# Where a sum over three chunks stands among the products of the following chunk, in the dense stage of a decoder layer

## The chip, the cores and the metric

The kernel runs as one program on 1 core of a Trainium2 chip. The metric is the device time of one execution in microseconds (us), lower is better. The engines are named as the profile names them: PE is TensorE (PEld its weight load), DVE is VectorE, ACT is ScalarE, POOL is GpSimd and SP is SyncE, which issues most of the transfers. Each engine works through its own instructions in the order in which they stand there.

## The reference

A decoder layer over 1024 tokens of width 1024: two attention-like mixers, and then a product-key expert layer, which is the part that matters here. For each token 8 heads pick 16 of 16384 experts each; every expert is one row of a table `u` and one row of a table `v`.

```python
u_sel = jnp.take(u_tab, idx, axis=0)                # rows of the chosen experts
h = jnp.einsum('bthkd,btd->bthk', u_sel, xb)
a = (jax.nn.gelu(h.astype(jnp.float32)) * g).astype(xb.dtype)
return jnp.einsum('bthk,bthkd->btd', a, jnp.take(v_tab, idx, axis=0))
```

## The kernel before

The tokens are 8 blocks of 128. A first part (to about 1490 us) does the mixers and chooses the experts. The rest, to which the change belongs, does the expert layer in two ways side by side.

**Fetched blocks.** For 3 of the blocks (5, 6, 7) `fetch` gathers the rows of the chosen experts from the tables (an indirect DMA that POOL issues, L954), and DVE does one instruction of 128x1024 on each (L992 for `u`, L979 for `v`). These steps are dealt out along the dense work by `pace`.

**Dense blocks.** For the other 5 blocks (640 tokens) every expert is computed, and a gate, zero for the experts that were not chosen, multiplies the result. The 16384 experts are 128 chunks of 128. For chunk `c`:

- `split_u` and `split` bring in the chunk's rows of `u` and `v` (`raw`, 512 KB each, 3 buffers, issued by SP on L845), and write each as a rounded high part (`uh`, `vh`: ACT, L846) and a low part (`ul`, `vl`: POOL, L847; DVE for the first chunks). A `raw` buffer is free again when POOL has made the low part. There are 2 buffers for `u` and `CH + 1` = 4 for `v`.
- `products` multiplies `u` with the tokens (`dhT`, held in full) into two PSUM tiles `h` of 320 tokens each: the two halves. Each is 24 matmuls of 128x320 (8 pieces of the contraction, and three matmuls high-high, high-low, low-high for each, L138 to L140). There are 3 buffers for `h`.
- `gated` does gelu (ACT, L116), the multiplication with the gates (DVE, L897; the gates come in as `gg` and `gw`, issued by SP on L875 and L885), and the split into `ah` (ACT, L899) and `al` (DVE, L900). It is written one chunk later than the products that it reads.
- `outs` is the sum: for three chunks (`CH = 3`) at a time, `ah`, `al` of 5 token blocks times `vh`, `vl`, in 10 PSUM tiles `yo` of 128x512 with 3 buffers, 9 matmuls each (three for each chunk, the last chunk's three last), and DVE adds each tile to `y` (L911). The buffers of `v` of the three chunks are free when the last tile is done.

The order of the instructions on each engine is not the order of the text. A scheduler lays it out ahead of time from its own picture of when things are ready; the order of the text says only who goes first where several are ready. POOL alone keeps the order of the text (`manual_schedule`).

In what follows a *sum* is `outs` of one group of three chunks, and the *last chunk* of a group is the one whose products end last: chunks 2, 5, ..., 125.

Of the kernel before, what the change touches and what calls it, by code (L numbers as in the profile page):

```python
# [55 lines left out]
def layer(ctx: ExitStack, tc: tile.TileContext, a: dict, out: bass.AP):  # L56
# [79 lines left out]
    def mm3(o, l, r, start, stop):  # L136

        T.matmul(o, l[0], r[0], start=start, stop=False)  # L138
        T.matmul(o, l[0], r[1], start=False, stop=False)  # L139
        T.matmul(o, l[1], r[0], start=False, stop=stop)  # L140
# [22 lines left out]
    def main():  # L163
# [139 lines left out]
        def group(b0, b1):  # L303
# [322 lines left out]
            def build(b, jf, gg):  # L626
# [36 lines left out]
                for t1 in range(0, P, TB):  # L663
                    hot = hp.tile([P, 4, TB // 2, P, 2], BF16, name="hot", tag="zs", bufs=NZS)
                    io = iota.unsqueeze(1).to_broadcast([P, TB // 2, P, 2])
                    of = lambda k: part[:, k, t1:t1 + TB].rearrange("p (a i) -> p a i", i=2).unsqueeze(2) \
                        .to_broadcast([P, TB // 2, P, 2])
                    V.tensor_tensor(hot[:, 0], io, of(1), op=OP.is_equal)
                    V.tensor_tensor(hot[:, 3], io, of(0), op=OP.is_equal)
                    for u in range(3):  # L670
                        V.tensor_tensor(hot[:, 1 + u], hot[:, 3], of(2 + u), op=OP.mult)
                    made.append((t1, hot))
                    if len(made) == NZS:
                        products()
                    yield 1.0
                while made:
                    products()
                    yield 0.0
# [132 lines left out]
        with ExitStack() as g:  # L811
            nbd = len(DENSE)
            CH = 3
# [20 lines left out]
            def pace(cost):  # L834
                nonlocal due
                due += cost
                while due > 0:
                    due -= PACE
                    next(side, None)

            def split(pool, name, src, bufs, E=G):
                raw = wp.tile([P, D], F32, name="raw", bufs=3)
                hi = pool.tile([P, D], F32R, name=name + "h", bufs=bufs)
                lo = pool.tile([P, D], F32R, name=name + "l", bufs=bufs)
                DQ.dma_start(raw, src)  # L845
                step["split"] = A.copy(hi, raw).ins.name  # L846
                E.tensor_sub(lo, raw, hi)  # L847
                return hi, lo

            def split_u(c):  # L850
                hi, lo = split(wp, "u", a["peer_uT"][c].rearrange("p k e -> p (k e)"), 2, V if c < AHEAD else G)
                return [t.rearrange("p (k e) -> p k e", e=P) for t in (hi, lo)]

            def products(u):

                halves = []
                for t0 in range(0, ND, TH):
                    p = ps.tile([P, 512], F32, name="h", bufs=3)[:, 0:TH]
                    for k in range(KT):
                        mm3(p, (u[0][:, k], u[1][:, k]),  # L860
                            (hT[0][:, k, t0:t0 + TH], hT[1][:, k, t0:t0 + TH]), k == 0, k == KT - 1)
                    halves.append(p)
                return halves

            wide = {}

# [36 lines left out]
            def outs(parts):  # L903
                for b in range(nbd):
                    bs = slice(b * P, (b + 1) * P)
                    for f in range(2):
                        p = ps.tile([P, 512], F32, name="yo", bufs=3)
                        ds = slice(f * 512, f * 512 + 512)
                        for u, ((ah, al), (vh, vl)) in enumerate(parts):
                            mm3(p, (ah[:, bs], al[:, bs]), (vh[:, ds], vl[:, ds]), u == 0, u == len(parts) - 1)  # L910
                        V.tensor_tensor(y[:, b, ds], y[:, b, ds], p, op=OP.add)  # L911
                        pace(0.65 * len(parts))

            u = split_u(0)
            parts, last = [], None
            for c in range(NKEY + 1):
                if c < NKEY:
                    v = split(up, "v", a["peer_v"][c * P:(c + 1) * P], CH + 1, V if c < AHEAD else G)
                    un = split_u(c + 1) if c + 1 < NKEY else None
                    p = products(u)  # L920
                    u = un
                if c == 0:
                    for b in range(nbd):
                        DQ.dma_start(y[:, b], d_x1[DENSE[b]])
                if last is not None:
                    parts.append((gated(c - 1, last[0]), last[1]))
                if c < 2:
                    for _ in islice(first, None if c else H):
                        pass
                last = (p, v)  # L930
                pace(1.4 * nbd)
                if len(parts) == CH:
                    outs(parts)
                    parts = []
            if parts:
                outs(parts)
            for b in range(nbd):
# [6 lines left out]
    def fetch(blocks, decode, row, ahead, pool, bank):  # L944
# [20 lines left out]
        for b, table in work:  # L965
# [41 lines left out]
            had[b] = h  # L1007

    main()


# [56 lines left out]
```

## Time and profile before

| | us |
|---|---|
| median of 3 runs | 3417.93 (3412.2 to 3424.95) |
| the profiled execution, its own time | 3410.79 |
| its span, first to last instruction | 3409.0 |
| PE busy in the span | 3211.9 (94%) |
| DVE busy | 2665.7 (78%) |
| POOL busy | 2191.6 (64%) |
| ACT busy | 1296.9 (38%) |

Matmuls are pipelined: a record lasts longer than the distance to the start of the next one, so a busy PE is not PE at its peak, and the distance from start to start is what one matmul costs in a row of them. The granted clock (PEclk) is a share of the full 2.4 GHz. A wait is put down to the engine that released it last.

### The profile page before, as it was taken

The page shows a single profiled execution, that of the slowest core. Times are in us where ns is not written, and L with a number is a line of the kernel's source. Part 1 is how long each engine was busy: PE and PEld are TensorE (multiplying, and loading weights), DVE is VectorE, ACT ScalarE, POOL GpSimd, SP SyncE. Part 2 cuts the span into 40 slices and gives each one's busy share as a digit, 9 for nine tenths or more (in the row PEclk, how much of TensorE's full clock was granted, in tenths as well). Part 3 has the DMA queues.
Part 4 walks back from the last instruction along what each step waited for, and adds up shares of the span by engine and source line. Part 5 has one row for each costly group of instructions (what it writes and reads, how often), then busy time and mean ns, then how long its engine had stood idle before and what let it go on. Part 6 is the DMA issues. An engine that isn't in the chain of part 4 may idle for free.

```text
span 3409.0 us, 56377 instructions
## 1 busy us (share of the span) xinstructions
PE 3211.9 (94%) x20194; PEld 2936.4 (86%) x20194; DVE 2665.7 (78%) x6080; ACT 1296.9 (38%) x2440; POOL 2191.6 (64%) x1514
## 2 busy tenths in 40 slices
PE   7899999999889999978999999999999999999999
PEld 7799988999877899877888898888888888888887
DVE  5746996557997787899887878777787777778877
ACT  5565465554466755321222222222222222222221
POOL 3353177887888874015777767676767777777774
PEclk9999999999999999989999999999999999999999
DMA  7787555777645399667888889898889888888986
GB/s 218 214 243 254 168 135 124 152 169 171 129 77 119 68 182 183 169 244 261 319 297 303 302 310 323 300 330 296 320 304 328 316 307 317 315 311 321 327 303 240
DMA packets 625305, 832.81 MB, mean 244 GB/s; under 512 B 226176, under 2 KB 467456, under 8 KB 625024
## 3 DMA queue, kind: packets, MB, share of 16 engines
q1 hardware_dynamic: 459136, 426.29, 40.7%
q0 software_dynamic: 165888, 402.92, 36.7%
q8 instruction: 158, 2.59, 0.3%
q14 instruction: 123, 1.01, 0.1%
HBM read 757.03 MB, written 72.02 MB: 243 GB/s over the span
## 4 chain that ended last, share of the span: by engine, by line
PE 52%; DVE 17%; POOL 11%; DMA 7%; issue 7%; ACT 2%; another core or an unknown queue 0%; SPq 0%; POOLq 0%; DVEq 0%; ACTq 0%
POOL d_G L773 8%; PE yo L140 5%; PE yo L138 5%; PE h L140 5%; PE h L138 5%; PE yo L139 5%; PE h L139 5%; PE mm L138 5%; PE mm L139 5%; PE mm L140 4%; DVE row L992 4%; DVE g_p L979 3%; DMA raw<-in_peer_v 3%; POOL row L954 2%; DVE y L911 2%
## 5 line engine op out<-in xcount | busy, mean ns | idle before, releaser
L773 POOL DMA_INDIRECT d_G<-g_gate,g_idx x384 | 727.1, 1894 | 235.2 <-issue 114.2
L138 PE MATMUL h<-dhT,uh 128*128 128x320 f32 x2048 | 640.7, 313 | 26.3 <-ACT uh L846 15.4
L140 PE MATMUL h<-dhT,ul 128*128 128x320 f32 x2048 | 631.1, 312 | 15.2 <-POOL ul L847 9.3
L139 PE MATMUL h<-dhT,uh 128*128 128x320 f32 x2048 | 639.2, 312 | 0.0
L954 POOL DMA_INDIRECT row<-in_peer_u,g_idx x384 | 365.8, 953 | 422.0 <-ACT uh L846 190.6
L138 PE MATMUL yo<-vh,ah 128*128 128x512 f32 x1280 | 504.3, 399 | 61.7 <-ACT ah L899 42.9
L979 DVE SCALAR_TENSOR_TENSOR g_p<-row,g_h,g_p 128x1024 f32<-128x1024 f32 x384 | 492.7, 1283 | 48.3 <-DMA row<-in_peer_v,g_idx 41.3
L139 PE MATMUL yo<-vl,ah 128*128 128x512 f32 x1280 | 503.9, 396 | 1.6 <-POOL vl L847 1.6
L954 POOL DMA_INDIRECT row<-in_peer_v,g_idx x384 | 361.0, 940 | 218.1 <-DVE g_p L979 127.4
L992 DVE SCALAR_TENSOR_TENSOR row<-row,g_p 128x1024 f32<-128x1024 f32 x384 | 461.3, 1214 | 50.2 <-DMA row<-in_peer_u,g_idx 36.3
L140 PE MATMUL yo<-vh,al 128*128 128x512 f32 x1280 | 488.6, 394 | 0.0
L236 DVE TENSOR_TENSOR wl<-raw,wh 128x512 fp32r<-128x512 f32 x440 | 312.6, 713 | 192.9 <-ACT wh L235 179.8
L235 ACT CAST wh<-raw 128x512 fp32r<-128x512 f32 x528 | 326.1, 620 | 335.8 <-PE mm L140 101.4
L138 PEld LDWEIGHTS h<-dhT,uh 128*128 128x128 f32 x2048 | 391.5, 191 | 41.2 <-ACT uh L846 15.5
L140 PEld LDWEIGHTS h<-dhT,ul 128*128 128x128 f32 x2048 | 388.9, 191 | 24.4 <-POOL ul L847 11.0
L139 PEld LDWEIGHTS h<-dhT,uh 128*128 128x128 f32 x2048 | 391.2, 191 | 7.3
L911 DVE TENSOR_TENSOR y<-y,yo 128x512 f32<-128x512 f32 x430 | 287.7, 682 | 118.2 <-PE yo L140 72.9
L847 POOL TENSOR_TENSOR vl<-raw,vh 128x1024 fp32r<-128x1024 f32 x125 | 302.1, 2417 | 88.9 <-ACT vh L846 87.1
L138 PEld LDWEIGHTS yo<-vh,ah 128*128 128x128 f32 x1280 | 242.0, 190 | 119.5 <-ACT ah L899 48.3
L899 ACT CAST ah<-h 128x320 fp32r<-128x320 f32 x256 | 108.9, 426 | 529.4 <-DVE h L897 285.1
L847 POOL TENSOR_TENSOR ul<-raw,uh 128x1024 fp32r<-128x1024 f32 x125 | 301.3, 2411 | 7.4 <-ACT uh L846 7.4
L140 PEld LDWEIGHTS yo<-vh,al 128*128 128x128 f32 x1280 | 241.8, 190 | 49.1
(239 smaller groups left out, 7046.2 us busy)
## 6 DMA issues: line engine op xcount, KB each, us to landing
raw<-in_w_in SPq DMA_DIRECT2D x312, 256.0 KB
raw<-in_peer_uT SPq DMA_DIRECT2D x128, 512.0 KB
raw<-in_peer_v SPq DMA_DIRECT2D x128, 512.0 KB
d_G<-zero SPq DMA_DIRECT2D x24, 1024.0 KB
raw<-in_peer_w_q SPq DMA_DIRECT2D x96, 256.0 KB
d_B<-sl SPq DMA_DIRECT2D x32, 512.0 KB
gg<-d_G SPq DMA_DIRECT2D x128, 128.0 KB
gw<-d_B SPq DMA_DIRECT2D x32, 512.0 KB
```

What stands on the lines that cost most here:

```text
L138: T.matmul(o, l[0], r[0], start=start, stop=False)
L139: T.matmul(o, l[0], r[1], start=False, stop=False)
L140: T.matmul(o, l[1], r[0], start=False, stop=stop)
L235: A.copy(hi, raw)
L236: on["lo"][0](lo, raw, hi)
L773: d = G.indirect_dma_start(out=d_G[g], out_offset=bass.IndirectOffsetOnAxis(ap=to[:, s:s + 1], axis=0), in_=gg[:, s:s + 1], in_offset=None ...
L847: E.tensor_sub(lo, raw, hi)
L899: A.copy(ah[:, t], q)
L911: V.tensor_tensor(y[:, b, ds], y[:, b, ds], p, op=OP.add)
L954: d = G.indirect_dma_start(out=t, out_offset=None, in_=a["peer_v" if u else "peer_u"], in_offset=bass.IndirectOffsetOnAxis(ap=g_idx[b][:, ...
L979: V.scalar_tensor_tensor(acc, t, h[:, s:s + 1], acc, op0=OP.mult, op1=OP.add)
L992: V.scalar_tensor_tensor(t, t, 1.0, x, op0=OP.mult, op1=OP.mult, accum_out=h[:, s:s + 1])
```

## The change

`products` becomes a generator that gives out one half at a time. In the loop over the chunks the sum of a full group stood at the end of a pass, behind all of that chunk's products and the gating. It now stands in the next pass, between the first half of that chunk's products and the issue of that chunk's `v` and the next chunk's `u`; the second half follows them. Nothing is computed that was not computed before.

```diff
             def products(u):
-                halves = []
                 for t0 in range(0, ND, TH):
                     p = ps.tile([P, 512], F32, name="h", bufs=3)[:, 0:TH]
                     for k in range(KT):
                         mm3(p, (u[0][:, k], u[1][:, k]),
                             (hT[0][:, k, t0:t0 + TH], hT[1][:, k, t0:t0 + TH]), k == 0, k == KT - 1)
-                    halves.append(p)
-                return halves
+                    yield p
...
             for c in range(NKEY + 1):
                 if c < NKEY:
+                    half = products(u)
+                    p = [next(half)]
+                    if len(parts) == CH:
+                        outs(parts)
+                        parts = []
                     v = split(up, "v", a["peer_v"][c * P:(c + 1) * P], CH + 1, V if c < AHEAD else G)
                     un = split_u(c + 1) if c + 1 < NKEY else None
-                    p = products(u)
+                    p += list(half)
                     u = un
...
                 last = (p, v)
                 pace(1.4 * nbd)
-                if len(parts) == CH:
-                    outs(parts)
-                    parts = []
             if parts:
                 outs(parts)
```

What the scheduler makes of it is shown at three places. Lines of the changed kernel from L853 on are two lower (`gg` L873, `ah` L897).

The first is PE behind the products of chunk 80, the last chunk of its group (`h_29753` is its second half; `h_29813`, `h_29838` and, after, `h_29801`, `h_29838` are the halves of chunk 81; `ah_29868` belongs to chunk 80). Before:

```order
L140 MATMUL h_29753<-dhT0_18841,ul_29639 128x320
L138 MATMUL h_29813<-dhT0_18841,uh_29723 128x320 [waits DVE_49]
L139 MATMUL h_29813<-dhT1_18842,uh_29723 128x320
L140 MATMUL h_29813<-dhT0_18841,ul_29724 128x320 [waits Pool_49]
...
L138 MATMUL h_29838<-dhT0_18841,uh_29723 128x320 [waits DVE_49]
...
L140 MATMUL yo_29888<-vh_29632,al_29782 128x512
L138 MATMUL yo_29888<-vh_29717,ah_29868 128x512 [waits Activation_49]
```

After:

```order
L140 MATMUL h_29753<-dhT0_18841,ul_29664 128x320
L138 MATMUL h_29801<-dhT0_18841,uh_29748 128x320 [waits DVE_49,Activation_49]
L139 MATMUL h_29801<-dhT1_18842,uh_29748 128x320
L138 MATMUL yo_29913<-vh_29742,ah_29868 128x512 [waits Activation_49]
L139 MATMUL yo_29913<-vl_29743,ah_29868 128x512 [waits Pool_49]
...
L138 MATMUL h_29838<-dhT0_18841,uh_29748 128x320 [waits DVE_49]
L139 MATMUL h_29838<-dhT1_18842,uh_29748 128x320
L140 MATMUL yo_29913<-vh_29742,al_29869 128x512
...
L140 MATMUL h_29801<-dhT0_18841,ul_29749 128x320 [waits Pool_49]
```

The first matmul that needs `ah` of chunk 80 stood behind both halves of chunk 81; it now stands behind two matmuls of chunk 81.

The second is SP at the same place (`gg_30087` is the gates of chunk 81, the `raw` of `in_peer_v` next to it the `v` of chunk 81). Before:

```order
L845 DMA raw_29722<-in_peer_uT 128x1024 [waits DMAHW1_49,Pool_49]
L845 DMA raw_29801<-in_peer_v 128x1024 [waits DMAHW4_49,Pool_49]
L875 DMA gg_30087<-d_G0_131 128x256 [waits DMAHW3_49,DMAHW2_49,DVE_49]
L875 DMA gg_30087<-d_G1_132 128x128
L885 DMA gw_30482<-d_B_133 128x2x512 [waits DVE_49]
```

After:

```order
L845 DMA raw_29747<-in_peer_uT 128x1024 [waits DMAHW1_49,Pool_49]
L873 DMA gg_30087<-d_G0_131 128x256 [waits DMAHW3_49,DMAHW2_49,DVE_49]
L873 DMA gg_30087<-d_G1_132 128x128
L883 DMA gw_30482<-d_B_133 128x2x512 [waits DVE_49]
L845 DMA raw_29826<-in_peer_v 128x1024 [waits DMAHW4_49,Pool_49]
```

The load of `v` of chunk 81 moved behind three loads of gates that wait for DVE.

The third is ACT at chunk 104, also the last of its group (`vh` is that of chunk 105; `h_32890`, after `h_32878`, is the first half of chunk 104, `ah_33030` what becomes of it). Before:

```order
L846 CAST uh_32885<-raw_32884 128x1024 [waits DMAHW1_49,Pool_49]
L899 CAST ah_32943<-h_32830 128x320 [waits DVE_49,Activation_49]
L846 CAST vh_32964<-raw_32963 128x1024 [waits DMAHW3_49]
L116 ACTIVATE h_32890<-h_32890 128x320 [waits PE_49]
L899 CAST ah_33030<-h_32890 128x320 [waits DVE_49]
```

After:

```order
L897 CAST ah_32943<-h_32830 128x320 [waits DVE_49,Activation_49]
L846 CAST uh_32910<-raw_32909 128x1024 [waits DMAHW1_49,Pool_49]
L116 ACTIVATE h_32878<-h_32878 128x320 [waits PE_49]
L846 CAST vh_32989<-raw_32988 128x1024 [waits DMAHW5_49]
L897 CAST ah_33030<-h_32878 128x320 [waits DVE_49]
```

Gelu of chunk 104 moved ahead of the cast of `vh`, and the cast to `ah` still stands behind it.

## Rows read from the trace of the kernel before

**Rows 1.** The page: its first line.

```profile
span 3409.0 us, 56377 instructions
```

**Rows 2.** Windows: stretch, its us, busy us of each engine, PEclk, DMA share, GB/s.

```profile
1754.00:3409.00 1655.00, 1588.92 (x8738) 1433.85 (x8736) 1283.59 (x1935) 421.63 (x688) 1165.79 (x896) 0.99 0.86 309
```

**Rows 3.** Waits of PE, 1754 to 3409: us in total, times, longest.

```profile
PE yo L138 <- ACT ah L899: 37.2, 16, 5.9
```

**Rows 4.** Timeline of PE, chunk 98: start, us, line; in brackets idle before, releaser.

```profile
2949.66 0.39 PE L140 MATMUL yo<-vh,al 128*128 128x512 f32 x1
...
2963.12 0.31 PE L138 MATMUL h<-dhT,uh 128*128 128x320 f32 x1
2963.27 0.31 PE L139 MATMUL h<-dhT,uh 128*128 128x320 f32 x1
2966.65 0.96 PE L138 MATMUL yo<-vh,ah 128*128 128x512 f32 x3 [3.07 <-ACT ah L899]
```

**Rows 5.** Timeline of POOL, the same place.

```profile
2949.94 2.42 POOL L847 TENSOR_TENSOR vl<-raw,vh 128x1024 fp32r<-128x1024 f32 x1 [2.12 <-ACT vh L846]
2952.31 2.41 POOL L847 TENSOR_TENSOR ul<-raw,uh 128x1024 fp32r<-128x1024 f32 x1
```

**Rows 6.** Timeline of SP (issues of transfers), the same place.

```profile
2956.42 0.80 SPq L875 DMA_DIRECT2D gg<-d_G  x2
2957.32 0.37 SPq L845 DMA_DIRECT2D raw<-in_peer_v  x1
```

**Rows 7.** Timeline of ACT, the same place.

```profile
2964.24 1.04 ACT L846 CAST vh<-raw 128x1024 fp32r<-128x1024 f32 x1 [5.68 <-DMA raw<-in_peer_v]
2965.19 0.42 ACT L116 ACTIVATE h<-h 128x320 f32<-128x320 f32 x1
2966.18 0.42 ACT L899 CAST ah<-h 128x320 fp32r<-128x320 f32 x1 [0.57 <-DVE h L897]
```

**Rows 8.** Timeline of PE, chunk 80.

```profile
2682.60 0.39 PE L140 MATMUL yo<-vh,al 128*128 128x512 f32 x1
...
2705.84 0.40 PE L138 MATMUL yo<-vh,ah 128*128 128x512 f32 x1
2706.07 0.39 PE L139 MATMUL yo<-vl,ah 128*128 128x512 f32 x1
```

**Rows 9.** Timeline of ACT, chunk 80.

```profile
2694.28 1.05 ACT L846 CAST vh<-raw 128x1024 fp32r<-128x1024 f32 x1 [2.27 <-DMA raw<-in_peer_v]
...
2697.60 0.42 ACT L899 CAST ah<-h 128x320 fp32r<-128x320 f32 x1 [1.94 <-DVE h L897]
```

**Rows 10.** Timeline of PE, the first and the last of 37 groups (chunks 17 and 125).

```profile
1754.31 0.39 PE L140 MATMUL yo<-vh,al 128*128 128x512 f32 x1
...
3342.86 0.39 PE L140 MATMUL yo<-vh,al 128*128 128x512 f32 x1
```

**Rows 11.** Timeline of ACT, the same two groups.

```profile
1767.34 0.43 ACT L899 CAST ah<-h 128x320 fp32r<-128x320 f32 x1 [1.55 <-DVE h L897]
...
3356.13 0.42 ACT L899 CAST ah<-h 128x320 fp32r<-128x320 f32 x1 [0.56 <-DVE h L897]
```

**Rows 12.** Timeline of SP, chunk 80.

```profile
2687.61 0.33 SPq L845 DMA_DIRECT2D raw<-in_peer_v  x1
2689.81 0.80 SPq L875 DMA_DIRECT2D gg<-d_G  x2
2691.52 0.37 SPq L885 DMA_DIRECT2D gw<-d_B  x1
```

**Rows 13.** Timeline of PE, chunk 41.

```profile
2121.46 0.50 PE L138 MATMUL yo<-vh,ah 128*128 128x512 f32 x1 [0.93 <-ACT ah L899]
```

**Rows 14.** Windows behind the waits at chunks 41, 98 and 53 (columns as in rows 2).

```profile
2121.30:2125.00 3.70, 3.54 (x19) 3.15 (x20) 3.67 (x6) 1.88 (x4) 3.08 (x4) 1.00 0.90 296
2966.60:2970.00 3.40, 3.35 (x11) 2.85 (x12) 3.40 (x9) 1.38 (x2) 3.07 (x3) 0.70 0.86 292
2304.40:2308.00 3.60, 3.47 (x9) 2.89 (x10) 3.05 (x8) 1.78 (x4) 2.16 (x1) 0.50 0.76 279
```

**Rows 15.** Waits of ACT, 1754 to 3409.

```profile
ACT vh L846 <- PE yo L140: 173.7, 16, 12.7
```

## The prediction

> **What bounds the kernel now.** I first placed the change in the span [rows 1]: it concerns the dense stage, from about 1490 us to the end. The windows view of that stage from chunk 17 on [rows 2] shows PE with a matmul in flight for 1588.9 of 1655 us, at a granted clock of 0.99. The DMA engines are 0.86 busy, DVE 78% (1283.6 of 1655) and POOL 70%. So PE sets the time, and time can be won or lost only where PE idles or runs slowly. The waits view [rows 3] names the largest idle: 37.2 us, 16 times, the first matmul that needs `ah` of a group's last chunk.
>
> Then I followed one such wait back, at chunk 98. The previous sum's last matmul starts at 2949.66 and is over at 2950.05 [rows 4]. That frees the buffers of `v`, and a chain starts. POOL makes `vl` and then `ul` (2.42 and 2.41 us), done at 2954.72 [rows 5]. That frees a `raw` buffer for the next `v`, but SP first issues a load of gates that waits until 2956.42, and the load of `v` goes out at 2957.32 [rows 6]. ACT sits before its cast of that `v` until 2964.24; gelu of chunk 98 stands behind the cast in ACT's order and starts at 2965.19; `ah` is there at 2966.60 [rows 7]. From the end of one sum to `ah`, the chain takes 16.55 us. Meanwhile PE had only 61 matmuls of 128x320 and 18 of 128x512 to do. Their spacings are 0.147 us (0.15 in rows 4) and 0.228 us (0.23 in rows 8), so 61 x 0.147 + 18 x 0.228 = 13.1 us of work. Chain less work is 3.5 us; the row shows 3.07 idle [rows 4], since a record of a matmul outlasts the spacing by some 0.4 us here.
>
> At chunk 80 there is no wait. The sum before ends at 2682.99, and `ah` is needed only at 2705.84 [rows 8], since both halves of chunk 81 (48 matmuls) stand between. The chain of 15.03 us (`ah` done at 2698.02 [rows 9]) is hidden by 23.05 us of work. Of the 37 groups from chunk 17 to chunk 125 the order before has 13 with such room (24 matmuls or more of the next chunk in front) and 24 tight ones (two matmuls).
>
> **The change part by part.** It adds no instruction and takes none away. POOL's order is the same row by row. What moves is PE, SP, ACT and DVE, by the scheduler.
>
> *PE.* In the text the sum now stands behind half of the next chunk's products. In PE's order it does not: the place at chunk 80 shows `ah` needed behind two matmuls of the next chunk, and this is so in 36 of the 37 groups. (The rest of the next chunk's first half waits for `ul` in the scheduler's picture, so the sum slips in ahead.) The 13 groups with room become tight. To price it I took each of the 37 chains of the trace, from the end of the sum before to the end of `ah`, and set the work that the new order puts into it against it. The first: 1754.70 to 1767.77, a chain of 13.07 us [rows 10, 11]; 66 + 18 matmuls before, 13.81 us, no wait; 55 + 18 after, 12.19 us, a wait of 0.9. The last: 3343.25 to 3356.55, 13.30 us; 12.63 us of work before, so 0.7 of wait; 13.95 after, none. Chunk 80: 12.92 us after against 15.03, a wait of 2.1. Over all 37 this gives 77 us. The same arithmetic with the old order gives 44.5 us, which is the 37.2 of rows 3 and some 0.45 for each of its 16 waits, so the arithmetic reproduces what was measured. Difference: **+33 us**. In 4 groups gelu moves ahead of the cast of `vh`, with `ah` still behind it, as shown at chunk 104: the chain is shorter there by the gelu and the multiplication, 1 us (2965.19 to 2966.18 [rows 7]), **-4 us**. Bounds of this part: -37 if no wait on `ah` is left, and +33 if the swap on ACT is worth nothing.
>
> *SP.* In 19 of the 37 groups the load of the next `v` is newly behind one to three loads of gates (chunk 80 is one); these wait until DVE has used the gates of two chunks ago. At chunk 80 the load went out at 2687.61, and the gates at 2689.81 and 2691.52 [rows 12]: behind them the load would be 4.3 us later, and so would all of the chain. Taken in this way, over the 19, it is 51 us of chain, 50 us of wait. That is the upper bound. The lower bound is zero, as the tight groups of before have the load behind the gates already (chunk 98, 2.6 us lost on SP [rows 5, 6]), and their chains are on average no longer (15.1 us in both sorts). I take +8, nearer to the row-for-row comparison of chains than to the issue times, because the gates come free earlier once those groups are tight.
>
> *Clock.* Behind the short wait at chunk 41 (0.93 us [rows 13]) the granted clock stays at 1.00; behind the waits at chunks 98 and 53 it is 0.70 over 3.4 us and 0.50 over 3.6 us [rows 14], PE's lower level of 1.2 GHz for part or all of the stretch. That costs 1.0 and 1.8 us of full-speed time. Of the waits in the arithmetic above, 8 come out longer than about 2.5 us with the old order and 13 with the new. 5 more at 1.0: **+5 us** (to +37, if all 36 tight groups paid it). The Trainium skill, page "TensorE: Matmul & The Clock Gate", section "HAM oscillation — how this bites in real kernels", describes a kernel that waits for a transfer once per tile and starts each tile at the slow clock. By that every tight group would pay, the +37; the row at chunk 41 speaks against it.
>
> *DVE.* The additions to `y` of the first three tiles move ahead of `al` of the second half. DVE is not the bound, and `al` is needed 44 matmuls, 6.5 us, later; three additions are 2 us. Zero. The new place of `al` of the first half, needed 8 matmuls behind the first use of `ah`, is covered too: `al` comes about 1.1 us behind `ah`, the matmuls in between take 1.7. What it costs if that cover goes: some tenths for each group, 10 us at most.
>
> *Sum.* 33 - 4 + 8 + 5 = +42 us. On the profiled execution that is 3410.8 + 42 = 3453 us. Its own time lies 7.1 us under the median of the runs (3417.93), so on the scale of the medians it is **3460 us**, 1.2% slower.
>
> **The rivals.**
>
> *The chains shorten when PE waits (no change).* The longest piece of a chain is the transfer of `v`, 6.7 us from issue to cast at chunk 80 [rows 9, 12], with the DMA engines 0.86 busy [rows 2]. If PE waits, the other users of the transfers and DVE's backlog catch up, and the next chain is shorter. If all of the 42 us is given back so, 3418, within 17 us either way. For it: the transfers are the second busiest resource of the stage. Against it: the chain of a group that follows a tight one is 15.3 us on average, not shorter than the others.
>
> *Gelu of the middle chunk comes earlier (faster).* Before, in 17 groups ACT has the casts of `vh` that wait for the end of the sum ahead of gelu of the group's middle chunk; ACT sits there for 173.7 us in 16 waits [rows 15]. After, gelu stands first in all groups, so DVE gets its work earlier, its backlog behind the sum is smaller, and the gates come free before SP asks for them. It decides from the point where the mean chain falls from 15.1 below the 13.2 us of work: then the waits on `ah` go, 37 us, 3374 on the profiled scale and **3381** on that of the medians. Against it: POOL's and SP's 4.7 us and the transfer are untouched by that, and they alone make up 11 to 12 us.
>
> *Everything waits (worse).* The loads behind the gates cost what chunk 80 suggests: 33 - 4 + 50 + 20 for the clock = +99, **3517** on the scale of the medians.
>
> *The sum does not move.* That the scheduler leaves things as they are is excluded by the order: 13 groups with room become one.
>
> **How the numbers follow.** My forecast, more waits on `ah`, 0.60: around 3460. Worse, 0.10: around 3510. No change, 0.21: 3418. Faster, 0.09: around 3381. The range should leave out no more than 2 in 10: the faster case and the far end of the worse one, so 3408 to 3505. What a measurement can tell from no change is about 0.5%, 17 us: below 3401 faster, above 3435 slower. Slower 0.70, the same 0.21, faster 0.09.
>
> **What would show it.** In the profile after, the wait of PE for `ah` in 1754 to 3409 should be about 65 to 75 us and in 25 or more places instead of 37.2 in 16; the granted clock 0.97 to 0.98 instead of 0.99; at chunk 80 the load of `v` behind the gates on SP, and an idle PE for 2 to 6 us ahead of the sum. The wait of ACT for the end of the sum should shrink, without PE gaining from it. I am wrong if the wait for `ah` is no longer than before (then the chains shortened, and the rows of SP and ACT at a tight group say where), or if it grows and the time does not (then something other than PE sets the time).

## The result

| | us |
|---|---|
| before, median of 4 runs | 3420.51 (3412.2 to 3424.95) |
| after, median of 4 runs | 3456.55 (3452.31 to 3461.07) |
| ratio after to before | 1.0115, 95% interval 1.0091 to 1.0139 |
| span of the profiled execution, before and after | 3409.0 and 3453.3 |

The changed kernel is 1.15% slower. The first line of its page, the same window as in rows 2 (its end moved by the 44 us), and the waits of TensorE in it, which answer to rows 3:

```profile
span 3453.3 us, 56428 instructions
```

```profile
1754.00:3453.00 1699.00, 1611.47 (x8767) 1446.16 (x8765) 1295.60 (x1948) 421.46 (x689) 1168.56 (x897) 0.98 0.85 302
```

```profile
PE yo L138 <- ACT ah L897: 67.2, 23, 6.5
PE yo L138 <- DVE y L909: 10.9, 19, 1.5
PE h L140 <- POOL ul L847: 2.7, 5, 0.7
```

The wait for `ah` went from 37.2 us in 16 places to 67.2 us in 23. The granted clock of the stretch went from 0.99 to 0.98. Of the 44 us by which the span grew, 30 stand in one row. The granted clock of the whole span, before and then after:

```profile
core 0: 3409.0 us, clock 0.970
core 0: 3453.3 us, clock 0.966
```

What is missing to the full clock is 102 us of the span before and 117 us after; so the lower clock costs some 15 us more, an estimate from these two lines. The other waits of TensorE together shrank by some 8 us.

Not all of the 44 us lie in the 37 groups of the prediction. The first product of the dense stage before, then after, and the end of the sum before chunk 17 after (before: [rows 10]):

```profile
1490.73 0.64 PE L138 MATMUL h<-dhT,uh 128*128 128x320 f32 x1 [15.36 <-ACT uh L846]
```

```profile
1490.06 0.63 PE L138 MATMUL h<-dhT,uh 128*128 128x320 f32 x1 [15.42 <-ACT uh L846]
...
1762.67 0.39 PE L140 MATMUL yo<-vh,al 128*128 128x512 f32 x1
```

From the first product to the end of that sum it is 264.0 us before and 273.0 after; from there to the last instruction 1654.3 and 1690.2. So some 9 of the 44 us are lost ahead of the 37 groups and 36 in them.

One place in full: chunk 80, which had room before ([rows 8, 9, 12]). TensorE, SyncE, GpSimd and ScalarE of the changed kernel there, and a window over the 3.6 us behind the wait (columns as in rows 2):

```profile
2712.61 0.39 PE L140 MATMUL yo<-vh,al 128*128 128x512 f32 x1
...
2725.98 0.31 PE L139 MATMUL h<-dhT,uh 128*128 128x320 f32 x1
2731.71 0.80 PE L138 MATMUL yo<-vh,ah 128*128 128x512 f32 x1 [5.43 <-ACT ah L897]
```

```profile
2718.25 0.80 SPq L873 DMA_DIRECT2D gg<-d_G  x2
2719.96 0.37 SPq L883 DMA_DIRECT2D gw<-d_B  x1
2720.43 0.41 SPq L845 DMA_DIRECT2D raw<-in_peer_v  x1
```

```profile
2715.27 2.40 POOL L847 TENSOR_TENSOR ul<-raw,uh 128x1024 fp32r<-128x1024 f32 x1
```

```profile
2729.30 1.04 ACT L846 CAST vh<-raw 128x1024 fp32r<-128x1024 f32 x1 [7.90 <-DMA raw<-in_peer_v]
2730.25 0.42 ACT L116 ACTIVATE h<-h 128x320 f32<-128x320 f32 x1
2731.23 0.43 ACT L897 CAST ah<-h 128x320 fp32r<-128x320 f32 x1 [0.57 <-DVE h L895]
```

```profile
2731.60:2735.20 3.60, 3.49 (x9) 2.91 (x10) 3.60 (x5) 1.34 (x3) 3.37 (x2) 0.52 0.79 316
```

The sum before ends at 2713.0. GpSimd has freed the `raw` buffer at 2717.67. SyncE stands at the gates and issues the load of `v` only at 2720.43. It is cast from 2729.30, gelu follows in ScalarE's order, and TensorE idles 5.43 us. Behind the wait it runs at a granted 0.52, the lower level for nearly all of the 3.6 us.

### The profile page after: what moved, and what is told of

Same layout as the page of the kernel before. It is cut to its first block, busy times and chain, and to the rows that moved or that the text cites. A ratio compares the mean times of both kernels' runs of the same rounds, so it can differ in the third digit from the quotient of the medians.

```text
span 3453.3 us, 56428 instructions
## 1 busy us (share of the span) xinstructions
PE 3229.1 (94%) x20194; PEld 2945.0 (85%) x20194; DVE 2677.4 (78%) x6080; ACT 1297.0 (38%) x2440; POOL 2207.3 (64%) x1514
## 4 chain that ended last, share of the span: by engine, by line
PE 34%; DVE 23%; POOL 16%; issue 12%; DMA 10%; ACT 3%; another core or an unknown queue 1%; SPq 0%; POOLq 0%; DVEq 0%; ACTq 0%
POOL d_G L773 12%; DVE row L993 5%; DVE g_p L980 4%; DMA raw<-in_peer_v 4%; PE yo L140 3%; PE yo L138 3%; PE mm L138 3%; PE h L140 3%; PE mm L139 3%; PE mm L140 3%; PE h L138 3%; PE yo L139 3%; PE h L139 3%; POOL row L955 2%; DVE y L909 2%
## 5 line engine op out<-in xcount | busy, mean ns | idle before, releaser
L773 POOL DMA_INDIRECT d_G<-g_gate,g_idx x384 | 740.6, 1929 | 233.6 <-issue 115.9
L140 PE MATMUL h<-dhT,ul 128*128 128x320 f32 x2048 | 629.2, 313 | 10.9 <-DVE ul L847 5.8
L993 DVE SCALAR_TENSOR_TENSOR row<-row,g_p 128x1024 f32<-128x1024 f32 x384 | 461.1, 1214 | 30.8 <-DMA row<-in_peer_u,g_idx 20.1
L138 PEld LDWEIGHTS h<-dhT,uh 128*128 128x128 f32 x2048 | 392.9, 192 | 42.6 <-ACT uh L846 15.6
L897 ACT CAST ah<-h 128x320 fp32r<-128x320 f32 x256 | 109.3, 427 | 751.2 <-DVE h L895 338.8
```

The costliest lines, as they stand in the source:

```text
L773: d = G.indirect_dma_start(out=d_G[g], out_offset=bass.IndirectOffsetOnAxis(ap=to[:, s:s + 1], axis=0), in_=gg[:, s:s + 1], in_offset=None ...
L897: A.copy(ah[:, t], q)
L993: V.scalar_tensor_tensor(t, t, 1.0, x, op0=OP.mult, op1=OP.mult, accum_out=h[:, s:s + 1])
```

## The experiments

Three things could have made the wait longer: TensorE's order (no room between the sum before and the first use of `ah`), SyncE's order (the load of `v` behind the gates), and ScalarE's order (gelu behind the cast of `v`), which hands the first two on. Each rule below is an edge for the scheduler that names instructions of one engine alone and adds no wait. The scheduler then lays out the other engines anew, apart from GpSimd, whose order is the same in all kernels; so no run changes one order and nothing else. What each run has at the three places, in how many of the 37 groups, counted in the traces (room: 24 or more matmuls of the next chunk ahead of the first use of `ah`):

| | room on TensorE | load of `v` ahead of the loads of `gg` on SyncE | `ah` ahead of the cast of `v` on ScalarE |
|---|---|---|---|
| before | 13 | 17 | 0 |
| after | 1 | 2 | 1 |
| before_room | 37 | 7 | 1 |
| after_half | 37 | 0 | 0 |
| after_act | 1 | 2 | 37 |
| before_act | 14 | 17 | 37 |
| after_sp | 0 | 37 | 1 |
| before_sp | 10 | 37 | 1 |
| after_sp19 | 1 | 17 | 1 |
| after_actsp | 0 | 37 | 37 |
| before_actsp | 9 | 37 | 37 |
| after_gg3 | 1 | 0 | 1 |
| before_roomact | 37 | 7 | 37 |

All ratios are to the kernel before on the same chip, with 95% intervals. The chips differ (the kernel before took 3403.7 to 3420.5 us on them), so ratios compare across runs and times do not.

### Room for all: before_room

In the kernel before, each matmul of a sum that needs the group's last chunk stands behind the last product that the text has issued so far:

```diff
-                            mm3(p, ..., u == len(parts) - 1)
+                            m = mm3(p, ..., u == len(parts) - 1)[0]
+                            if u == CH - 1:
+                                tc.add_manual_dep(m.ins, step["product"], order, reason="room")
```

> The kernel before, with one more rule for the order on TensorE alone: the sum's first matmul that needs the group's last chunk stands behind all products of the following chunk. All 37 groups then have room (19 to 21 us of work against chains of 11.6 to 20.4). If the room decides, the wait of TensorE for ah from chunk 17 on falls from 37 us to under 4, the slow clock behind the long waits goes with it (8 us), and the time is about 3375 us, 0.987 of before. Rival, the chain of transfers sets the pace: the wait comes back in another place (the low parts ul, the buffers of yo) and the time stays within 3405 to 3420.

Measured: 3437.2 us, **1.0086** (1.0056 to 1.0117). Slower than before. Waits of TensorE from 1754 us on:

```profile
PE h L138 <- DVE al L902: 67.5, 25, 7.3
PE yo L138 <- DVE y L916: 9.9, 11, 5.3
```

The wait for `ah` is gone from the list. In its place stands one for `al`, by products. The last chunk's halves hold two of the three PSUM buffers of `h` until `al` is made; the second half of the next chunk needs the first of them. At chunk 81 it looks like this:

```profile
2720.00 0.64 PE L138 MATMUL h<-dhT,uh 128*128 128x320 f32 x1 [6.08 <-DVE al L902]
```

So the rival held, in a form that neither side had named and with a time above its range (3405 to 3420): the late gelu has two customers, the sum and the next products' buffer, and room for the one is no room for the other. That the products in front of the sum are the main price, as I had it, is refuted.

### The sum where the text puts it: after_half

The same edge in the changed kernel, where the last product issued so far is the first half that the text puts ahead of the sum.

> The changed kernel, with the sum held where its text puts it: the first matmul that needs the group's last chunk stands behind the first half of the products that precede it in the text. If the lost room is what the change cost, the 67 us of waiting for ah go, with some 13 us of slow clock: about 3376 us, 0.987 of before. Rival, the later place in the text costs by itself (the buffers of v come free later, the low parts ul are late): 3430 to 3456, with TensorE waiting for ul or vl instead.

Measured: 3557.0 us, **1.0437** (1.0405 to 1.0469), far outside both expectations. Waits of TensorE:

```profile
PE yo L138 <- DVE y L914: 55.6, 87, 2.4
PE h L138 <- DVE al L900: 46.3, 53, 4.5
PE h L140 <- POOL ul L847: 35.6, 36, 2.3
```

Nothing waits for `ah`, and the other waits grow: the tiles of the sum stand close together (between the first use of `ah` and the end of the sum 24 matmuls of products on average, 81 in the changed kernel) and wait for VectorE to free `yo`, the products for `al` and for `ul`. That the scheduler did not follow the text was no loss: the order that the text asks for, as this edge enforces it, is worse than either kernel.

### Gelu first: after_act and before_act

On ScalarE the cast of the next `v` stands behind gelu and the cast to `ah` of the last chunk's first half. For this, `gated` is written ahead of the issue of `v`; the rest stays.

```diff
-                step["split"] = A.copy(hi, raw).ins.name
+                cast = A.copy(hi, raw)
+                if behind_ah:
+                    tc.add_manual_dep(cast.ins, behind_ah, order, reason="gelu first")
...
+                    if last is not None:
+                        parts.append((gated(c - 1, last[0]), last[1]))
                     v = split(up, "v", a["peer_v"][c * P:(c + 1) * P], CH + 1, V if c < AHEAD else G,
+                              step["ah", 0] if c > AHEAD and c % CH == 0 else None)
```

> The changed kernel, TensorE's order as tight as in it; on ScalarE alone the cast of the next v stands behind gelu and the cast to ah of the group's last chunk's first half. If the wait for ah is the wait for the load of v, handed on by ScalarE's order, the 67 us shrink to under 15 though there is no more room than before: about 3385 us, 0.99 of before. Rival, room alone counts, and ah is late for other reasons (DVE's backlog): 3440 to 3456.

> The kernel before, with the cast of the next v behind gelu and ah of the group's last chunk on ScalarE. If the wait for ah is the load of v handed on by ScalarE, the 37 us of before go too, with their slow clock: 0.987 to 0.99 of before, and the room of TensorE is then worth little, so this is near the changed kernel with the same rule (0.9946). Rival, room still counts: it is 25 us better than that one, 0.987 or less.

Measured: after_act 3384.4 us, **0.9946** (0.9930 to 0.9961); before_act 3368.7 us, **0.9896** (0.9865 to 0.9927). The first wait of TensorE in each:

```profile
PE yo L138 <- ACT ah L900: 18.0, 6, 6.2
```

```profile
PE h L138 <- DVE al L903: 15.9, 9, 5.1
PE yo L138 <- ACT ah L902: 7.7, 4, 4.4
```

With TensorE as tight as in the changed kernel (13.4 us of work on average, against 13.3), the wait falls from 67.2 to 18.0 us and 1.7% of the time goes. The load of `v` is no earlier in after_act: it goes out 1.6 us after its buffer is free on average, against 1.1 in the changed kernel. This shows the link: `ah` is late because gelu stands behind a cast that waits for a transfer. The wait was to fall below 15 us and the ratio to 0.99, so a part of it has other grounds. The two runs differ by 0.5%, some 17 us; the intervals allow 5 to 29, so the 25 that I gave to room are not excluded.

### The load of v first: after_sp, before_sp, after_sp19

On SyncE the loads of gates stand behind the load of `v` of the same chunk: in all groups of the changed kernel, in all groups of the kernel before, and in the changed kernel only in the 19 groups, from chunk 20 on, in which the change had turned them round.

```diff
-                DQ.dma_start(raw, src)
+                step["load", name] = DQ.dma_start(raw, src).ins.name
...
                         load = DQ.dma_start(gg[:, at:at + n], ...)
+                        tc.add_manual_dep(load.ins, loads[c], order, reason="v first")
```

> The changed kernel, TensorE's order as tight; on SyncE alone the loads of gates stand behind the load of v of the same chunk, in all groups. The load of v loses 1.1 us a group to the gates in the trace after (41 us over 37 groups). By the sum of the prediction this term is worth about 8 us: about 3448. Rival, the order of the loads is the cause: up to 37 us of waiting go and 5 us of slow clock, about 3414 us. A third outcome: the gates come late and the multiplication waits for them, 3460 or more.

> The kernel before, with the load of v ahead of the loads of gates on SyncE in all groups, as in the run of the changed kernel with that order (0.9955 of before). The two then differ by TensorE's order alone (16.1 us of work against 13.2 in front of the first use of ah). If the room that the change took is worth what the prediction says, about 25 to 30 us, this one is 0.987 to 0.988. If SyncE's order is the whole cause, it is equal to the other: 0.9955.

> The changed kernel, TensorE's order as tight; on SyncE the loads of gates stand behind the load of v only in the 19 groups in which the change had put them ahead, so that SyncE's order is about that of before. By the prediction's terms (8 us of 42 on SyncE) 1.009 of before. By the run with all groups turned round (54 us for 37 groups), 19 groups are worth about 28 us: 1.003. If SyncE's order is all of the change's cost: 1.000.

| | us | ratio | 95% interval |
|---|---|---|---|
| after | 3456.6 | 1.0115 | 1.0091 to 1.0139 |
| after_sp19 | 3418.5 | 1.0038 | 1.0019 to 1.0056 |
| after_sp | 3392.2 | 0.9955 | 0.9941 to 0.9969 |
| before_sp | 3365.6 | 0.9884 | 0.9854 to 0.9913 |

The first wait of TensorE, from 1754 us on, in after_sp19, after_sp and before_sp:

```profile
PE yo L138 <- ACT ah L903: 50.2, 22, 6.4
```

```profile
PE yo L138 <- ACT ah L899: 25.3, 18, 5.8
```

```profile
PE yo L138 <- ACT ah L901: 13.8, 7, 4.3
```

At chunk 80 of after_sp the load goes out at 2680.14, 0.02 us after GpSimd has freed the buffer:

```profile
2680.14 0.33 SPq L845 DMA_DIRECT2D raw<-in_peer_v  x1
2681.37 0.80 SPq L873 DMA_DIRECT2D gg<-d_G  x2
```

Three things follow. The change's part on SyncE is 1.0115 less 1.0038, 0.8% or some 26 us (the intervals allow 16 to 37), not 8; after_sp19 was to be at 1.003 if so, and after_sp, by its rival, at 3414 us; 0.9955 is 3405 on that scale. These 26 us are not the price of SyncE's order alone for certain, since VectorE's order and a little of TensorE's were laid out anew too. What is left with SyncE put back, 1.0038 against 1, and with the load first in both kernels, 0.9955 against 0.9884, is 0.4 to 0.7%, 13 to 24 us: TensorE's order, with what moved on VectorE and, in up to 5 groups, on ScalarE. And the order of the loads was bad before the change too: before_sp is 1.2% faster than the kernel before.

How much of the rest is room lost in the 37 groups stays open. The end of the sum before chunk 17 and the first line of the page, of after_sp19 (with its first product of the dense stage ahead), after_sp and before_sp:

```profile
1500.23 0.63 PE L138 MATMUL h<-dhT,uh 128*128 128x320 f32 x1 [15.20 <-ACT uh L846]
...
1774.07 0.39 PE L140 MATMUL yo<-vh,al 128*128 128x512 f32 x1
span 3427.9 us, 56432 instructions
```

```profile
1767.63 0.39 PE L140 MATMUL yo<-vh,al 128*128 128x512 f32 x1
span 3392.7 us, 56464 instructions
```

```profile
1749.47 0.39 PE L140 MATMUL yo<-vh,al 128*128 128x512 f32 x1
span 3352.6 us, 56422 instructions
```

From there to the end after_sp19 takes 1653.4 us, as long as the kernel before (1654.3): the longer wait for `ah`, 50.2 against 37.2 us, is made up for by shorter ones for `ul`, `al` and `yo`. Its loss lies ahead of the 37 groups: 274.2 us from its first product, 264.0 before. With the load first, the kernel without room takes 1624.7 us from there on and the one with 1602.7. So by one execution each, the room lost in these groups cost between nothing and 22 us, depending on the order of the loads.

### Both rules: after_actsp and before_actsp

> The changed kernel with both rules, ScalarE's and SyncE's. The wait for ah was 18 us with the first and 25 with the second from chunk 17 on. If both cut the same wait, the second adds little to the first: 0.993 to 0.9946 of before. If they add up, the wait is nearly gone: 0.988 to 0.99.

> The kernel before with both rules, ScalarE's (0.9896 alone) and SyncE's (0.9884 alone). The first left 8 us of waiting for ah and 16 for al, the second 14 for ah. If they cut the same wait, as on the changed kernel (0.9921 for both, 0.9946 and 0.9955 alone), the two together bring little more: 0.985 to 0.989.

Measured: after_actsp **0.9921** (0.9894 to 0.9949), before_actsp 3378.2 us, **0.9891** (0.9852 to 0.9929). The second rule adds nothing that can be told on the kernel before, and at most a little on the changed one: the wait for `ah` is 15.9 us in after_actsp and 11.3 us in before_actsp, against 18.0, 25.3, 7.7 and 13.8 with one rule. Both rules take the same wait out of the same chain. The version that beats both kernels is the kernel before with one of the rules; before_sp and before_act can't be told apart.

### A third buffer for the gates: after_gg3

```diff
-                    gg = up.tile([P, P * sum(map(len, strewn))], F32, name="gg")
+                    gg = up.tile([P, P * sum(map(len, strewn))], F32, name="gg", bufs=3)
```

> The changed kernel with a third buffer for the gates gg. SyncE's order is left as the scheduler lays it (the gates ahead of the load of v in all groups), TensorE's order is as tight. If the load of v is late because the gates ahead of it wait for a buffer, that wait goes with the third buffer and the time falls as with the order turned round: about 0.996 to 0.999 of before. If it is the order of the transfers itself (the gates' bytes go first), nothing changes: 1.01.

Measured: **1.0086** (1.0054 to 1.0119), the wait for `ah` 70.4 us. It tells nothing apart. The scheduler spent the buffer on issuing the gates one chunk earlier, so that SyncE still stands at them, here for 251.9 us against 274.5 in the changed kernel:

```profile
SPq L873 <- DVE h L895: 251.9, 78, 10.4
```

Whether the wait or the bytes of the gates hold up the load of `v` stays open for this reason.

### Room and gelu first: before_roomact

> The run with room forced in all groups (1.0086 of before) with ScalarE's rule added: gelu and ah of the last chunk ahead of the cast of the next v. In the run without that rule the 37 us of waiting for ah had turned into 67 us of waiting for al, at the second half of the next chunk, which needs the PSUM buffer that the late gelu holds. If the late gelu is the cause of both, that wait goes too, under 15 us, and the time is 0.985 to 0.99 of before. If the forced order itself costs (the sum too late for its followers), it stays above 1.0.

Measured: 3401.5 us, **0.9956** (0.9935 to 0.9977). This lies between the two expectations. The wait for `al` fell from 67.5 to 32.4 us, so the late gelu was half of it. The other half stays with the forced order, and the wait for `yo` grew from 9.9 to 20.1 us; what makes these two late no run shows:

```profile
PE h L138 <- DVE al L905: 32.4, 16, 6.6
PE yo L138 <- DVE y L919: 20.1, 21, 5.6
```

Compare before_act, the same rule without the forced room: 0.9896.

## Why the prediction was right, and where it was not

**The end, the bound and the mechanism: right; the sum: by luck.** 3460 was forecast and 3456.6 measured, inside the range. TensorE sets the time: of the runs that took waits off it, each became faster. The wait for `ah` was to be 65 to 75 us in 25 or more places; it is 67.2 in 23. At chunk 80 the load of `v` was to stand behind the gates with 2 to 6 us of idle; it was 5.43. The granted clock of 0.97 to 0.98 is 0.98. But the terms do not hold one by one: SyncE's is about three times too small, TensorE's too large, the clock's too small, and the 9 us ahead of the 37 groups stand in no term. That they add up to 42 is luck.

**TensorE's order, +33: right total, wrong ground.** The arithmetic gave 77 us of waiting over 37 groups with the old chains and 44.5 with the old order. Redone with its own spacings (0.147 and 0.228 us) on all 37 it gives 76 and 43, and 72 on the trace after, so the total is about right. But the old chains were not what the new order met. In the 19 groups whose loads moved on SyncE, the mean chain was 15.3 us before; with SyncE's order put back and TensorE tight (after_sp19) it is 14.4, and in the changed kernel 15.6. Two errors cancelled. Of the 15.3 us, 3.6 lie between the start of the cast of `v` and `ah`, against 2.7 in the other 18 groups: where nobody waits for `ah`, the multiplication can come late on VectorE at no cost, and the chain looks longer than it has to be. This slack is about a third of the fall to 14.4, as the piece is still 3.3 us in after_sp19; the rest lies ahead of the cast. Measured, this part is at most 13 to 24 us, and in the 37 groups between nothing and 22. At chunk 98 the prediction puts the 0.4 us between its 3.5 and the 3.07 idle down to the record of a matmul; by [rows 4] that accounts for 0.16 (a record of 0.31, a spacing of 0.15).

**SyncE, +8: the term that was mis-sized.** It is some 26 us. The step that failed is the one where I chose between the ends (0 and 50) by a comparison of mean chains, "15.1 us in both sorts" (15.1 and 15.3). The two sorts were not alike: 13 of the 17 groups with the load first were the ones with room, whose chains had the slack just told. The issue times at chunk 80 [rows 12] pointed the right way.

**ScalarE, -4.** At chunks 38, 50, 104 and 116 gelu did run ahead of the cast, and `ah` still stood behind it (at chunk 89 `ah` ran ahead too); no run tells what that was worth. The cast behind `ah` in all groups is worth 1.7%.

**Clock, +5: too small.** By the same arithmetic 13 waits were longer than 2.5 us, as expected. But the lower clock cost some 15 us more over the two spans, so the 1.0 us for each was too little: at chunk 80, 3.6 us at 0.52 cost 1.7. The long wait there was 5.43 us. The Trainium skill, page "TensorE: Matmul & The Clock Gate", section "HAM oscillation — how this bites in real kernels", describes a kernel whose waits of some 3 to 5 us are each followed by the slow clock; the trace agrees for the waits at chunks 80 and 98 (3.07 us). The 0.93 us at chunk 41 [rows 13, 14] are shorter than any wait told of there, so the prediction's +37, every tight group paying, does not follow from that section.

**VectorE, 0: right as far as it shows.** The waits for `yo` are 10.9 us; products wait for `al` for 0.3 us.

**The rivals.** That chains shorten when TensorE waits was half true, as the 14.4 us show, and SyncE's order ate it. The faster case had its cause half right: gelu of the middle chunk did move ahead, and the 173.7 us that ScalarE sat before casts of `vh` for the end of the sum [rows 15] are gone. But the wait moved to another instruction: the cast to `ah` of the middle chunk, of which there are 4 buffers, waits for the sum that still reads the oldest. Before, then after:

```profile
ACT ah L899 <- PE yo L139: 122.4, 16, 13.8
```

```profile
ACT ah L897 <- PE yo L139: 302.1, 31, 15.5
```

ScalarE stood at the end of the sum for 173.7 + 122.4 = 296.1 us in 32 waits before and for 302.1 us in 31 after. That this wait would shrink, as the prediction says, did not come true. The text's meaning (the sum half a chunk later) never reached the chip; after_half shows that it would have cost 4%.

## What to carry to other kernels

Where a scheduler lays out the order, read the order and not the text: this change moved the sum the other way than it says, and its cost came in good part from a load that swapped places on SyncE, an engine that seemed to have nothing to do with it. A chain that nobody waits for can have slack in it; its length is an upper bound and must not be compared with that of a chain that is waited for. Where the bounding engine waits for a short step on an idle engine, look at what stands ahead of that step in its queue: two edges, one on ScalarE and one on SyncE, were each worth over 1% of the kernel before. And an edge on one engine makes the scheduler lay out the others anew: count at all places what it did before a difference is put down to it.

## What was not expected of the hardware

A load that stood behind others on SyncE paid twice here. In the 13 groups that had room, the load of `v` took 6.1 us from issue to cast before, 7.1 after, with up to three loads of gates in front of it, and 5.8 with the load first again (after_sp). So beside the later issue, 1.5 us after its buffer is free (0.03 before), about 1 us is lost on the way, at 0.85 to 0.88 of the DMA engines busy in all of them. Whether the bytes of the gates ahead of it are the reason no run shows. The Trainium skill, page "Trainium Kernel Development and Optimization", section "Key Constraints", says that transfers from all issuing queues share the same 16 engines and that several issuers save only issue time; here issue time includes standing at a load whose buffer is not free, and that was dear. No run here issued from another engine.
